# First dot products 14 tiles later, the first three column tiles multiplied pass by pass over pairs of channel tiles, and the parameters loaded behind x

## The chip, the cores and the metric

The kernel runs on one core of a Trainium2 chip. The metric is the device time of one execution in microseconds (us); the times shown are medians of several executions. The engines named below are TensorE (PE, with its weight loads as PEld), VectorE (DVE), ScalarE (ACT), GpSimd (POOL) and SyncE (SP), which issues nearly all DMA transfers.

## What is computed

One inference step of a two-layer backbone over 640 tokens (128 of a prompt, 512 of a sample), width 1024. Cut to what the change touches:

```python
def trunk_layer(x, mod_vec, rope, init, l, p):
    shift, scale, gate = split(silu(mod_vec) @ w_mod[l] + b_mod[l], 3)
    h = rms_norm(x, norm_g[l]) * (1 + scale) + shift
    proj = h @ w_in[l]              # 92 column tiles of 128, and 16 columns ca/cb
    ...                             # four mixers, each forward and backward:
    #  A retention, B RG-LRU, C gated DeltaNet (cq ck cv cz ca cb), D HGRN2 (dq df di dz)
    yb = einsum(branches, w_branch[l])
    y = sum(sigmoid(mg) * yb) @ w_out[l]
    return x + gate * y             # and the mixers' final states
```

A final RMS norm follows the second layer. The prompt and the sample have a modulation vector each (`c_ctx`, `c`), so every channel has two values of shift, scale and gate.

## The kernel before

**Tiling.** Everything is held transposed: channels on the 128 partitions, 640 tokens along the free side. `h` is eight tiles of 128 channels (KD = 8). For precision each operand of a product is split in a high part, rounded to fp32r, and a low part, the rest: `hh`, `hl` for h, `whi`, `wlo` for a weight tile. A column tile of 128 output channels is then `hi·hh + hi·hl + lo·hh`, summed over the eight channel tiles in PSUM, in two halves of 384 and 256 tokens: 48 matmuls (`product`, L363 to L391). ACT makes `whi` (L360), DVE makes `wlo` (L361); the buffers for raw weights, high and low parts are two each.

**Jobs.** `layer_jobs` yields jobs, one for a column tile: first the small one of ca and cb (16 columns, two passes only, no low part), then ck, cq, cv, dq, df, df, di and so on. `drive` takes them in, up to three ahead, and runs them. Beside them run two lanes of mixer work, whose pieces the loop places by a clock of its own; gate tiles (mg) fill in and are written out to memory where the next mixer's tiles have no buffer.

**What sets the order.** The kernel's text gives each instruction a priority, the earlier the higher. A list scheduler with a model of the times then builds each engine's queue: of those instructions whose inputs are ready in the model and whose buffer has come round (the tiles of one tag are given out in the order of the text), an engine takes the earliest in the text. So a late instruction that is ready goes ahead of an early one that is not. On the chip each engine works its queue off in that fixed order. `issue_after`, `behind` and `Ordered` (whose instructions show line L104) add edges by hand: while `ordered('V', True)` holds, the DVE instructions of the text keep their order among themselves.

**The start.** `first_h` (L663 on) makes h of layer 0, in tokens of a hand-written order: `x` loads a tile of x and adds its square, `T` and `B` make the norm's factor, `l` loads eight tiles of modulation rows, `m` multiplies them on PE, `p` transposes the result on PE and computes two tiles' worth of shift and scale, `y` normalises a tile in place, `n` makes its high part on ACT (L650), `o` its low part on DVE, `P` computes constants from the parameters (`prepare`, some 55 small DVE operations in one chain, with a few ACT operations that wait for them). The head ends with y0 and y1; the rest stands in eight steps, one for each channel tile. The first three jobs (ca/cb, ck, cq) form a group that runs with these steps: after each step, the group's matmuls of that channel tile are issued for all three jobs. In the trace their PSUM tiles have the name `wide`. ca/cb gets the 1024-column tile, ck the two banks of tag `pj`, cq those of `m1`; the fourth job, cv, needs a bank of tag `pj`.

**The dots.** The gates of both layers and the shift and scale of layer 1 don't come from PE but from DVE: `mod_dots` (L607) loads two tiles of 128x512 of `w_mod` (`wm`, three buffers) and makes four multiply-and-sum operations (`mjunk`, L613), each with an accumulator read behind it. There are 24 such steps in layer 0 and 8 in layer 1, 128 dots in all. The first step calls `cond_silu` (L595), which loads the two vectors in four pieces (`cs<-in_cvec`) and needs four tiles of the mixers' tag `pu` (11 buffers) for their tanh (`cth`, L602, on ACT; L603 on DVE). `layer_jobs` takes one step of dots with every third job:

```python
EVERY, done = 3, 0
...
                done += 1
                if done % EVERY == 0:
                    next(extra, None)
                yield j
```

Of the kernel before, what the change touches and what calls it, by code (L numbers as in the profile page):

```python
# [79 lines left out]
def hybrid_kernel(ctx: ExitStack, tc: tile.TileContext, I, O):  # L80
# [89 lines left out]
    cs0 = cp.tile([128, KD, 2], F32, name="cs0")  # L170
    nc.sync.dma_start(cs0, I['ccol'])
    par = cp.tile([128, NPAR], F32, name="par")
    nc.sync.dma_start(par, I['params'])
    ident = cp.tile([128, 128], F32, name="ident")
    con = cp.tile([128, NCON], F32, name="con")
    lvm = cp.tile([128, 5, 32], U8, name="lvm")
# [128 lines left out]
    tick = [lambda: None]  # L305
    clock = [0.0]
    held = [0]
    wide, wide_step = [], []
    zout = [0, 0]

    def free(n, z=False):
# [34 lines left out]
    def split_w(j, raw, spare=False, lo_on=None, after=[]):  # L346
        if spare:
            hi, lo = Parts(), Parts(3 - int(spare))
            for i in range(2):
                r = raw[:, 4 * i:4 * i + 4]  # L350
                A.activation(hi.tiles[i], r, AF.Copy)
                V.tensor_sub(lo.tiles[i], r, hi.tiles[i].bitcast(F32))
            return hi, lo
        if j.m < 128:
            both = w_tile(j, F32R, "hi", 1)
            A.activation(both[:, :, :16], raw, AF.Copy)
            V.tensor_sub(both[:, :, 16:], raw, both[:, :, :16].bitcast(F32))
            return both, None
        hi, lo = w_tile(j, F32R, "hi", 2), w_tile(j, F32R, "lo", 2)
        A.activation(hi, raw, AF.Copy)  # L360
        behind(lambda: (lo_on or j.lo_on or V).tensor_sub(lo, raw, hi.bitcast(F32)), after)  # L361
        return hi, lo

    def product(hi, lo, rh, rl, evac, nk=8, k0=0, halves=HALVES, tag="pj", after={}):


        m = hi.shape[-1]

        def passes(ps, k, a, b):
            ops = ((hi, rh), (hi, rl), (lo, rh))[:3 if lo else 2]  # L370
            for n, (w, r) in enumerate(ops):
                PE.matmul(ps[:m, :b - a], w[:, k0 + k], r[k][:, a:b], start=(k + n == 0), stop=(k == nk - 1 and n == len(ops) - 1))  # L372
        if wide:
            pss = [wide.pop(0) for _ in halves]
            for k in range(nk):
                for (a, b), ps in zip(halves, pss):
                    passes(ps, k, a, b)
                yield
            for (a, b), ps in zip(halves, pss):
                evac(ps[:m, :b - a], a, b)  # L380
            return
        for a, b in halves:
            ps = psp.tile([128, 512], F32, tag=tag, name="pj", bufs=2)
            for k in range(nk):
                behind(lambda: passes(ps, k, a, b), [after[k]] if k in after else [])
                clock[0] += (3 if lo else 2) * (b - a) / 2400
                tick[0]()
            evac(ps[:m, :b - a], a, b)
            yield
# [9 lines left out]
    def drive(jobs, ahead):  # L399


        q = []
        more = True

        def prepare_next(i, spare=False, lo_on=None, after=[]):
            if len(q) > i and len(q[i]) == 2 and q[i][0].deep >= i:
                j, lo = q[i]
                q[i] = j, lo, split_w(j, lo, spare, lo_on, after)
                if j.prep:
                    j.prep()  # L410

        def fill(n):
            nonlocal more
            while more and len(q) < n:
                j = next(jobs, None)
                if j is None:
                    more = False
                elif j == 'flush':
                    break
                else:  # L420
                    x = j, load_w(j)
                    if j.urgent and len(q) > 1 and len(q[-1]) == 2:
                        q.insert(-1, x)
                    else:
                        q.append(x)
                    if j.pre:
                        j.pre()
        while True:
            fill(ahead + 1)
            for i in range(3):  # L430
                prepare_next(i)
            if q:
                j, _, w = q.pop(0)
                if j.group:
                    n = j.group
                    fill(n - 1)
                    runs = [j.run(*w)]
                    for i in range(n - 1):
                        prepare_next(i, lo_on=None if n < 3 or wide_step else V, after=[edge['v0']] if n == 3 and 'v0' in edge else [])
                    for i in range(n - 1):  # L440
                        j, _, w = q.pop(0)
                        runs.append(j.run(*w))
                    if wide_step:
                        x = psp.tile([128, 1024], F32, tag="m21", name="wide", bufs=1)
                        wide.extend((x[:, :512], x[:, 512:]))
                        for tag in 'pj m1'.split():
                            wide.extend(psp.tile([128, 512], F32, tag=tag, name="wide", bufs=2) for _ in range(2))
                        f = wide_step.pop()
                        for k in range(KD):
                            behind(lambda: [next(r) for r in runs], f(k))  # L450

                        fill(1)
                        prepare_next(0, 1)
                        for r in runs[1:]:
                            next(r, None)
                    for r in runs:
                        if n == OG and n < 3 and r is runs[-1]:
                            fill(2)
                            prepare_next(0)
                            prepare_next(1, 2)  # L460
                        next(r, None)
                    fill(ahead + 1)
                    for r in runs:
                        for _ in r:
                            pass
                else:
                    for _ in j.run(*w):
                        pass
            elif not more:
                return  # L470
# [191 lines left out]

    def first_h():  # L663

        head, steps = 'x0 x1 x2 x3 x4 x5 x6 x7 l0 T m0 B p0 y0 y1'.split(), \
            [s.split() for s in 'l1 l2 l3 n0 n1 o0 m1|o1 p1 y2 y3 w1|n2 n3 o2 m2|o3 p2 y4 y5 w2|n4 n5 o4 m3|o5 p3 y6 y7 w3|n6 n7 o6|o7 P'.split('|')]
        csil = sLt[:, :256].rearrange("p (k c) -> p k c", k=KD)
        V.memset(csil, 0.0)
        th = small_tile([128, KD, 2], "cth", 1)
        A.activation(th, cs0, AF.Tanh, scale=0.5)  # L670
        V.scalar_tensor_tensor(csil[:, :, 0:2], th, 1.0, cs0, op0=OP.add, op1=OP.mult)
        nc.sync.dma_start(ident, I['ident'])
        rows, stat, xs, hh, hl = {}, {}, {}, [], []
        pm = M2(1024)
        two = up.tile([128, 2, T], F32, tag="hcb", name="two", bufs=1)
# [1 line left out]
        def load_x(k):  # L677
            if not xs:
                stat['ss'] = U(name="ss", on=1)
            xs[k] = U(name="x0", on=2)  # L680
            nc.sync.dma_start(xs[k], I['xT'][k])
            sum_sq(xs[k], stat['ss'], len(xs) == 1)

        def rms():
            stat['dg'] = stream_stat(stat['ss'], NT, two[:, 0])
# [46 lines left out]
            late.append(h_low(0, k, xs[k], 0, T, hh[k], hl[k]).ins)  # L732

        def do(tok):
            {'x': load_x, 'T': lambda n: rms(), 'B': lambda n: rms_bc(), 'l': load_rows, 'm': shift_scale, 'p': columns,
             'y': norm_x, 'o': low_h,
             'n': high_h, 'P': lambda n: behind(prepare, [late[0], *late[-2:]])}[tok[0]](int(tok[1:] or 0))

# [769 lines left out]
    def layer_jobs(f, l, extra, after_half):  # L1508
# [45 lines left out]
        jobs = [j for k, i in order for j in inp[k](i, st[k][i])]  # L1554
        gate_jobs, branch_jobs, spill = f['merge_jobs']((0, 1, 3, 2))
        AHEAD = 2
        EVERY, done = 3, 0
        jobs += gate_jobs[:AHEAD]
        gate_jobs = gate_jobs[AHEAD:]
        while jobs or any(lanes) or any(threads):  # L1560
            need = held[0] + sum((lanes[n] or threads[n]) != [] and not zout[n] for n in range(2))
            r = [t[1] for n in range(2) for t in [runnable(n)] if t]
            if extra_jobs:
                j = extra_jobs.pop(0)
            elif jobs and need + jobs[0].cost <= NPU - (RS if gate_jobs else 0):
                j = jobs.pop(0)
            elif gate_jobs and len(gate_jobs) > 8 - AHEAD and need < NPU and not (r and min(r) <= clock[0]):
                gate_jobs.pop()
                j = spill(AHEAD + len(gate_jobs))
            else:  # L1570
                j = None
            if j:
                held[0] += j.cost
                done += 1
                if done % EVERY == 0:
                    next(extra, None)
                yield j
            else:
                r = [(t[1], n, t) for n in range(2) for t in [runnable(n)] if t]
                if r:  # L1580
                    step(*min(r, key=lambda x: x[:2])[1:])
                else:
                    yield 'flush'
# [224 lines left out]
```

## Time and profile before

| | us |
|---|---|
| median of three executions | 2085.4 (2082.83 to 2087.55) |
| profiled execution, its own time | 2088.14 |
| profiled execution, span of its trace | 2086.3 |
| PE busy in the span | 2027.3 |
| DVE busy | 1401.3 |
| ACT busy | 909.3 |

The time of an execution and the span of its trace differ by 1.84 us: the span runs from the first to the last instruction. PE is busy for nearly all of it, but not in its first 120 us: the page's strip of forty slices of 52 us shows PE at 6 and 7 tenths in the first two and at 9 or more later. So the table says what the kernel is made of, and the first tenth of the span has to be read by itself, stretch by stretch.

### The profile page before, as it was taken

Reading aid. Unit: us, or ns where it says so; the run is one execution under the profiler, and the core shown is the slowest. Engines: PE = TensorE matmul, PEld = TensorE weight load, DVE = VectorE, ACT = ScalarE, POOL = GpSimd, SP = SyncE. Lnnn points to the kernel's source line nnn. Section 1 sums busy time; section 2 is a strip of 40 time slices with the busy share of each in tenths; the row PEclk is TensorE's granted clock in tenths of the full one; section 3 lists DMA queues with packets and bytes.
Section 4 is the critical chain, followed back from the end, with each engine's and each line's share of the span. In section 5 each row is a group of like instructions: output and inputs, shape, how many; then the busy total and the mean of one; then the engine's idle time right before and its main releaser. Section 6 shows DMA issues by size and latency. Waiting matters only on the chain.

```text
span 2086.3 us, 42690 instructions
## 1 busy us (share of the span) xinstructions
PE 2027.3 (97%) x17362; PEld 1983.7 (95%) x17362; DVE 1401.3 (67%) x3164; ACT 909.3 (44%) x1940; POOL 75.6 (4%) x195
## 2 busy tenths in 40 slices
PE   6799999999999999999999999999999999999997
PEld 5789999999999999999989999999999999999997
DVE  6999767866766855447567746855784686552775
ACT  4343464454445444422344435453644554362221
POOL 0000000000000000000000000000000000000000
PEclk9999999999999999999999999999999999999999
DMA  8544423323233232456322322332322233243642
GB/s 322 177 149 159 136 93 95 93 72 110 87 94 105 74 110 85 160 172 194 135 80 84 95 82 80 99 99 77 122 83 87 79 115 94 95 156 113 216 126 96
DMA packets 133305, 245.25 MB, mean 118 GB/s; under 512 B 44068, under 2 KB 59124, under 8 KB 132980
## 3 DMA queue, kind: packets, MB, share of 16 engines
q1 hardware_dynamic: 131956, 239.90, 35.6%
q8 instruction: 136, 2.23, 0.5%
q10 hardware_dynamic: 1152, 2.62, 0.3%
q14 instruction: 61, 0.50, 0.1%
HBM read 205.20 MB, written 37.27 MB: 116 GB/s over the span
## 4 chain that ended last, share of the span: by engine, by line
PE 86%; DMA 6%; DVE 4%; ACT 2%; issue 1%; SPq 1%; POOL 0%; DVEq 0%; ACTq 0%; POOLq 0%
PE pj L372 71%; PE m L298 13%; PE m L302 2%; DMA R<-gc 1%; DMA wss<-in_w_ss 1%; DVE mjunk L613 1%; DMA wm<-in_w_mod 1%; DMA sW<-l_dr 1%; DVE wlo L361 0%; DMA l_dr<-at 0%; DMA cs<-in_cvec 0%; DVE cs L835 0%; DMA tab<-in_tables 0%; DMA x<-in_xT 0%; ACT whi L360 0%
## 5 line engine op out<-in xcount | busy, mean ns | idle before, releaser
L372 PE MATMUL pj<-hh,whi 128*128 128x256 f32 (+2 forms) x2896 | 915.8, 316 | 13.0 <-ACT p_df L504 10.3
L372 PE MATMUL pj<-hl,whi 128*128 128x256 f32 (+2 forms) x2896 | 905.6, 313 | 0.0
L372 PE MATMUL pj<-hh,wlo 128*128 128x256 f32 (+1 forms) x2880 | 899.5, 312 | 0.0
L372 PEld LDWEIGHTS pj<-hh,whi 128*128 128x128 f32 (+1 forms) x2896 | 549.0, 190 | 18.0 <-ACT p_df L504 10.8
L372 PEld LDWEIGHTS pj<-hl,whi 128*128 128x128 f32 (+1 forms) x2896 | 549.2, 190 | 1.5 <-DVE hl L104 0.3
L372 PEld LDWEIGHTS pj<-hh,wlo 128*128 128x128 f32 x2880 | 546.8, 190 | 1.4
L361 DVE TENSOR_TENSOR wlo<-wraw,whi 128x1024 fp32r<-128x1024 f32 x228 | 278.7, 1222 | 162.1 <-ACT whi L360 158.8
L360 ACT ACTIVATE whi<-wraw 128x1024 fp32r<-128x1024 f32 x230 | 243.4, 1058 | 325.9 <-PE pj L372 291.2
L372 PE MATMUL pj<-bl,whi 128*128 128x384 f32 (+1 forms) x512 | 158.3, 309 | 0.0
L372 PE MATMUL pj<-bh,whi 128*128 128x384 f32 (+1 forms) x512 | 158.0, 309 | 0.0
L372 PE MATMUL pj<-bh,wlo 128*128 128x384 f32 (+1 forms) x512 | 157.8, 309 | 0.0
L372 PEld LDWEIGHTS pj<-bh,whi 128*128 128x128 f32 x512 | 96.4, 188 | 0.0
L372 PEld LDWEIGHTS pj<-bh,wlo 128*128 128x128 f32 x512 | 96.3, 188 | 0.0
L372 PEld LDWEIGHTS pj<-bl,whi 128*128 128x128 f32 x512 | 96.2, 188 | 0.0
L504 ACT ACTIVATE mg<-pj 128x384 f32<-128x384 f32 (+1 forms) x128 | 54.9, 429 | 87.0 <-PE pj L372 83.2
L613 DVE SCALAR_TENSOR_TENSOR mjunk<-wm,cs 128x512 bf16<-128x512 f32 x128 | 87.6, 684 | 2.6 <-DMA wm<-in_w_mod 2.2
L372 PE MATMUL pj<-yl,whi 128*128 128x256 f32 (+1 forms) x256 | 78.9, 309 | 0.0
L372 PE MATMUL pj<-yh,whi 128*128 128x384 f32 (+1 forms) x256 | 78.7, 310 | 0.0
L372 PE MATMUL pj<-yh,wlo 128*128 128x256 f32 (+1 forms) x256 | 78.0, 309 | 0.0
L526 ACT ACTIVATE junk<-m 128x128 bf16<-128x128 f32 x160 | 44.3, 277 | 73.7 <-PE m L298 62.9
L947 DVE TENSOR_TENSOR sW<-sW,sLt 128x126 f32<-128x126 f32 (+22 forms) x248 | 62.7, 253 | 12.1 <-ACT hkst L1161 3.9
L949 DVE TENSOR_TENSOR sW<-sW 128x126 f32<-128x126 f32 (+22 forms) x248 | 62.6, 252 | 4.6
(394 smaller groups left out, 2916.9 us busy)
## 6 DMA issues: line engine op xcount, KB each, us to landing
wraw<-in_w_in SPq DMA_DIRECT2D x184, 512.0 KB
mg<-mg SPq DMA_DIRECT2D x96, 320.0 KB
wm<-in_w_mod SPq DMA_DIRECT2D x64, 256.0 KB
wraw<-in_w_branch SPq DMA_DIRECT2D x32, 512.0 KB
R<-gc SPq DMA_DIRECT2D x32, 320.0 KB
braw<-br SPq DMA_DIRECT2D x32, 320.0 KB
wss<-in_w_ss SPq DMA_DIRECT2D x32, 256.0 KB
wraw<-in_w_out SPq DMA_DIRECT2D x16, 512.0 KB
```

The source lines that it names most:

```text
L298: return PE.matmul(out, lhsT, rhs, **k)
L302: return PE.transpose(out, in_, idn)
L360: A.activation(hi, raw, AF.Copy)
L361: behind(lambda: (lo_on or j.lo_on or V).tensor_sub(lo, raw, hi.bitcast(F32)), after)
L372: PE.matmul(ps[:m, :b - a], w[:, k0 + k], r[k][:, a:b], start=(k + n == 0), stop=(k == nk - 1 and n == len(ops) - 1))
L504: A.activation(dst[:, a:b], ps, AF.Tanh, scale=0.5)
L526: A.activation(junk, src3[:, t, :], AF.Square, accum_out=ss[:, t:t + 1])
L613: V.scalar_tensor_tensor(junk, w, 1.0, cs[2 * g + a], op0=OP.mult, op1=OP.mult, accum_out=macc[l][:, c, 2 * g + a:2 * g + a + 1])
L947: V.tensor_tensor(tv, X3[:, :m, i:i + 1].to_broadcast([128, m, n]), L3[:, i:i + 1, i + 1:].to_broadcast([128, m, n]), op=OP.mult)
L949: V.tensor_tensor(X3[:, :m, i + 1:], X3[:, :m, i + 1:], tv, op=OP.subtract)
```

## The change

1. `done` starts at -14 in layer 0 (0 in layer 1), and no step of dots is taken while it is negative: the first is taken with the fourteenth job instead of the third, and `cond_silu` with it.
2. In the group of three, the steps are taken in pairs of channel tiles. After the first step of a pair the pass hi·hh is issued for both tiles and all three jobs, then the pass hi·hl; after the second step, behind the PE transpose that it names, the pass lo·hh. The jobs are started in the order ck, cq, ca/cb, so that ck gets the 1024-column tile, cq the `pj` banks and ca/cb the `m1` banks.
3. The low parts of ck's and cq's weights (`wlo`) are not made before the group begins but after the first pair's first two passes in the text, so behind h's low parts o0 and o1, and ahead of p1, y2, y3 in DVE's order by hand. The tokens are rearranged: both low parts of a pair in one step, and `m` at the beginning of the next.
4. The parameters (170 KB) and the identity (64 KB) are loaded by a new token `i` behind x7 and ahead of l0; they were ahead of x.

```diff
-    nc.sync.dma_start(par, I['params'])
...
-    wide, wide_step = [], []
+    wide, wide_step, lows = [], [], []
...
-        behind(lambda: (lo_on or j.lo_on or V).tensor_sub(lo, raw, hi.bitcast(F32)), after)
+        def low():
+            behind(lambda: (lo_on or j.lo_on or V).tensor_sub(lo, raw, hi.bitcast(F32)), after)
+        if wide_step:
+            lows.append(low)
+        else:
+            low()
...
         if wide:
             pss = [wide.pop(0) for _ in halves]
-            for k in range(nk):
-                for (a, b), ps in zip(halves, pss):
-                    passes(ps, k, a, b)
-                yield
+            ops = ((hi, rh), (hi, rl), (lo, rh))
+            for p in range(0, nk, 2):
+                for n, (w, r) in enumerate(ops):
+                    for k in (p, p + 1) if w else ():
+                        for (a, b), ps in zip(halves, pss):
+                            PE.matmul(ps[:m, :b - a], w[:, k], r[k][:, a:b], start=(k + n == 0),
+                                      stop=(k == nk - 1 and n == (2 if lo else 1)))
+                    yield
...
-                        for k in range(KD):
-                            behind(lambda: [next(r) for r in runs], f(k))
+                        for p in range(KD // 2):
+                            f(2 * p)
+                            for n in range(2):
+                                for r in runs[1:] + runs[:1]:
+                                    next(r)
+                            if p == 0:
+                                for x in lows:
+                                    x()
+                                lows.clear()
+                            edges = f(2 * p + 1)
+                            behind(lambda: [next(r) for r in runs], edges)
...
-        head, steps = 'x0 x1 x2 x3 x4 x5 x6 x7 l0 T m0 B p0 y0 y1'.split(), \
-            [s.split() for s in 'l1 l2 l3 n0 n1 o0 m1|o1 p1 y2 y3 w1|n2 n3 o2 m2|o3 p2 y4 y5 w2|n4 n5 o4 m3|o5 p3 y6 y7 w3|n6 n7 o6|o7 P'.split('|')]
+        head, steps = 'x0 x1 x2 x3 x4 x5 x6 x7 i l0 T m0 B p0 y0 y1'.split(), \
+            [s.split() for s in 'l1 l2 l3 n0 n1 o0 o1|m1 p1 y2 y3 w1|n2 n3 o2 o3|m2 p2 y4 y5 w2|n4 n5 o4 o5|m3 p3 y6 y7 w3|n6 n7 o6 o7|P'.split('|')]
...
-        nc.sync.dma_start(ident, I['ident'])
...
+        def load_params():
+            nc.sync.dma_start(par, I['params'])
+            nc.sync.dma_start(ident, I['ident'])
...
-        EVERY, done = 3, 0
+        EVERY, done = 3, 0 if l else -14
...
-                if done % EVERY == 0:
+                if done >= 0 and done % EVERY == 0:
```

## Rows read from the trace of the kernel before

**Rows 1.** The page, busy time, share of the span and instructions of each engine.

```profile
PE 2027.3 (97%) x17362; PEld 1983.7 (95%) x17362; DVE 1401.3 (67%) x3164; ACT 909.3 (44%) x1940; POOL 75.6 (4%) x195
```

**Rows 2.** Busy time by stretch: start and end, length, each engine, granted clock, DMA.

```profile
24.44:53.85 29.41, 24.98 (x287) 21.91 (x283) 24.86 (x63) 11.77 (x23) 1.87 (x11) 1.00 0.85 314
...
86.66:96.72 10.06, 0.00 (x2) 0.00 (x1) 9.50 (x42) 1.86 (x5) 0.00 (x0) 0.74 0.56 181
96.72:101.50 4.78, 4.78 (x15) 4.78 (x16) 4.78 (x29) 0.22 (x1) 0.00 (x0) 0.50 0.54 164
...
112.43:114.92 2.49, 0.00 (x0) 0.00 (x1) 2.49 (x8) 0.24 (x1) 0.00 (x0) 1.00 0.32 105
114.92:118.60 3.68, 3.68 (x39) 3.46 (x43) 3.58 (x12) 0.47 (x2) 0.00 (x0) 0.56 0.89 275
...
131.00:150.00 19.00, 17.04 (x186) 16.33 (x186) 18.30 (x49) 8.99 (x22) 1.01 (x5) 1.00 0.47 151
```

**Rows 3.** The waits of PE, first 60 us (total, times, longest).

```profile
PE wide L372 <- DVE hl L104: 2.4, 2, 1.3
PE wide L372 <- ACT hh L650: 1.9, 1, 1.9
PE pj L372 <- ACT p_ck L491: 1.4, 1, 1.4
```

**Rows 4.** The waits of all engines, 86 to 97 us.

```profile
PE pj L372 <- ACT p_df L504: 10.1, 1, 10.1
ACT scr L219 <- DVE scr L218: 6.0, 1, 6.0
```

**Rows 5.** The timeline of DVE: start, duration, line, operation, tiles.

```profile
51.89 0.91 DVE L104 MEMSET sLt<- 128x1024 f32 x1 [0.16 <-issue]
...
83.25 0.69 DVE L613 SCALAR_TENSOR_TENSOR mjunk<-wm,cs 128x512 bf16<-128x512 f32 x1
...
83.87 0.17 DVE L104 SCALAR_TENSOR_TENSOR scr<-scr,scr 128x16 f32<-128x16 f32 x1
...
102.05 0.16 DVE L104 TENSOR_SCALAR ghh<-par 128x2 f32<-128x2 f32 x1
```

**Rows 6.** The dots, 44 to 131 us: durations least/median/most, first, last.

```profile
L613 DVE SCALAR_TENSOR_TENSOR mjunk<-wm,cs x68: 627/685/694, 44.9 to 127.8; 128x512 bf16<-128x512 f32 x68
```

**Rows 7.** The loads of xn, tokens of x for the output tiles.

```profile
L1469 SPq DMA_DIRECT2D xn<-in_xT x8: 333/386/1745, 954.7 to 1035.6; - x8
```

**Rows 8.** The timeline of ACT: where the eleventh job is evacuated.

```profile
142.88 0.26 ACT L490 ACTIVATE p_cv<-pj 128x128 f32<-128x128 f32 x1
```

**Rows 9.** The timeline of DVE: low weight parts, first dot.

```profile
24.46 2.35 DVE L104 TENSOR_TENSOR wlo<-wraw,whi 128x1024 fp32r<-128x1024 f32 x2
...
44.90 0.68 DVE L613 SCALAR_TENSOR_TENSOR mjunk<-wm,cs 128x512 bf16<-128x512 f32 x1
```

**Rows 10.** The timeline of SP, and the chain that ended last.

```profile
1.20 0.42 SPq L173 DMA_DIRECT2D par<-in_params  x1
...
2.13 4.29 SPq L681 DMA_DIRECT2D x<-in_xT  x8
...
5.25 6.41 DMA x<-in_xT
...
29.31 5.34 DMA wss<-in_w_ss
```

**Rows 11.** The timeline of PE at full clock, two matmuls on.

```profile
80.00 0.33 PE L372 MATMUL pj<-hh,whi 128*128 128x384 f32 x1
80.17 0.33 PE L372 MATMUL pj<-hl,whi 128*128 128x384 f32 x1
```

**Rows 12.** Busy time by stretch, as in rows 2, while dots still run.

```profile
150.00:240.00 90.00, 90.00 (x728) 89.31 (x727) 87.69 (x248) 32.25 (x70) 1.72 (x4) 1.00 0.49 154
```

**Rows 13.** The timeline of DVE: two steps of the first triangular solve.

```profile
149.82 0.18 DVE L947 TENSOR_TENSOR sW<-sW,sLt 128x31 f32<-128x31 f32 x1
...
189.81 0.27 DVE L947 TENSOR_TENSOR sW<-sW,sLt 128x110 f32<-128x110 f32 x1
```

More of the change, by code (lines that the diff above doesn't have):

```diff
@@ L734, in do @@
         def do(tok):
-            {'x': load_x, 'T': lambda n: rms(), 'B': lambda n: rms_bc(), 'l': load_rows, 'm': shift_scale, 'p': columns,
+            {'x': load_x, 'i': lambda n: load_params(), 'T': lambda n: rms(), 'B': lambda n: rms_bc(), 'l': load_rows, 'm': shift_scale, 'p': columns,
              'y': norm_x, 'o': low_h,
```

## Prediction

> **What bounds the kernel now.** I read the page first: PE is busy for 97% of the span [rows 1], so apart from waits the kernel takes as long as its matmuls, and the change takes none away. What it can win is idle time of PE and time at the lower clock. Next I cut the first 160 us into stretches by busy time and granted clock [rows 2], then asked in each which wait ended last [rows 3, 4], and last read what VectorE (DVE) and ScalarE (ACT) did there [rows 5]. Four places matter.
>
> The products with h run from 24.44 to 53.85 us. Of these 29.41 us PE is busy for 24.98, so 4.43 us are idle [rows 2]: two waits for low parts of h, 2.4 us, and one for a high part, 1.9 us [rows 3]. Behind the group cv waits another 1.4 us for ck's evacuation to free a `pj` bank [rows 3].
>
> From 86.66 to 96.72 PE stands still for 10.06 us and comes back at a granted clock of 0.50, the lower of the two levels (1.2 of 2.4 GHz), for 4.78 us [rows 2]. The wait is for the evacuation of a df tile, which ACT could have done; but ACT, working its queue in order, stood 6.0 us at an exponential that waits for DVE, and then at another [rows 4]. The operand is the end of a chain of small DVE operations of 0.17 us. That chain is `prepare` and then the softplus of the gates, and it needs from 51.89 to 102.05 us [rows 5], because its next operation is never ready when the last one ends: DVE slips a dot of 0.69 us in between each time [rows 5]. By 131 us 68 of the 128 dots have run [rows 6], although the text gives most of them a place far later.
>
> From 112.43 to 114.92 PE waits 2.49 us more, for `g`, at the end of the same softplus chain, and again runs slowly afterwards, at a mean clock of 0.56 for 3.68 us [rows 2]. From 131 to 150 it idles for 19.00 - 17.04 = 1.96 us.
>
> **Dots later.** Priority alone moves nothing, since the scheduler takes whatever is ready. What holds the dots back is a buffer: `cond_silu` needs four tiles of tag `pu`, and a tag's tiles are given out in the order of the text. The trace bears that out: the loads of xn need only a buffer and are not issued before 954.7 us [rows 7]. With the fourteenth job three ahead, the four tiles come behind those of the eleventh job, cv of the second head, evacuated at 142.88 us now [rows 8], some 20 us earlier once the stalls below are gone. So dots begin near 120 us in place of 44.90 [rows 9].
>
> First stall: chain and softplus have no dots between them. Some 55 operations of 0.17 to 0.25 us and the lane's own work end by about 70 us, ahead of ACT's need. 10.06 us go, and the slow stretch: 15 matmuls in 4.78 us are 0.319 each, 0.17 at full clock [rows 2, 11], so 2.2 to 2.4 us; I take 4.78 x (1 - 0.50) = 2.4. Sum -12.5. If the model's queue puts those exponentials ahead of an evacuation again, some of it stays: bound -6.
>
> Second stall: -2.49 and 3.68 x (1 - 0.56) = 1.6, so -4.1; bound 0, if `g` is still late.
>
> The dots' new place: the 60 dots after 131 us stand beside 1.96 us of idle PE from 131 to 150 [rows 2] and none from 150 to 240, with DVE nearly full [rows 12]: 0.033 us each at most. At that rate 128 cost 4.2, so +2.2 net of the 1.96 already paid. Lower bound: +0 - 2.0 (they cost nothing). Upper: the 68 early dots stood beside 12.5 + 4.1 = 16.6 us, 0.24 each; 128 x 0.24 = 31, +29 net. I take the lower rate, because the later dots are those that ran beside the same mixers. Their 64 loads of `wm` and four of the vectors stay on SP's queue, and weight loads queue behind them there as they do now; that is in the rate. The four `cth` tiles take turns in a tag of 11 whose next tiles (ak, aq) wait behind them: each needs a tanh and a multiplication of dot size, so four times about 1.4 us, an estimate from the dot's 0.69 [rows 5]. Two PSUM banks of the running products hide it; uncovered it would be 5 to 6.
>
> **The group of three.** The 4.43 us of idle time have three causes. First PE waits about 1.3 us for hl [rows 3], which stands on DVE behind two wlo of together 2.35 us [rows 9]; the new order puts o0 and o1 first, and the two passes hi·hh and hi·hl need no wlo. The two later waits (1.9, and 2.4 - 1.3 = 1.1) come from the four vector operations of `cond_silu` and the first dots, which start at 44.90 [rows 9] in the midst of y6 and y7; they leave with the dots. So up to -4.43.
>
> The x transfers: par and the identity are two issues, 2.13 - 1.20 = 0.93 us [rows 10]; x's eight tiles, 2.62 MB, take 6.41 us, 409 GB/s [rows 10], so 234 KB are 0.6 us. I take -0.6 (0 to -0.93): the chain x, squares, norm, y, n begins that much earlier. The parameters are needed only after m0, so their later landing is hidden by l0's 2.1 MB; uncovered it would cost the same 0.6.
>
> A new wait: on DVE p1, y2, y3 now stand behind both wlo (2.35 us), and the pass lo·hh waits on PE for p1's transpose. PE has there the two passes, 24 matmuls or about 3.4 us, the rest of m1 and what of m2 has landed, against about 2 us for o0 and o1 and 2.35 for the wlo: +0.6 (0 to 2). Later pairs have 2.9 us of products and 2 us of m to cover 4 us of y, n, o, and I see no wait. Sum of the group: -4.4 (0 to -6).
>
> cv's first wait: cq, not ck, now holds the `pj` banks, and its evacuation stands behind ck's on ACT, 0.4 us later; but ca/cb, with no third pass, and ck are finished before the group ends, so their evacuations are over sooner. I take 0.9 us of wait instead of 1.4, -0.5 (+0.7 to -1.3).
>
> Where TensorE runs first after long idling, the clock matters. The stretch from 24.44 is at 1.00 throughout [rows 2], though PE waited at the start. The Trainium skill, "TensorE: Matmul & The Clock Gate", section "What's actually happening", says that the throttled clock is the default and that activity releases it. By that rule the first products, which now come earlier, would run at 1.2 GHz for a while. Priced as the stretch after the second stall, 1.6 us, the rule would make the sum -17.7; the row, 1.00, doesn't bear it out, and the sum goes without it.
>
> **The sum.** -12.5 - 4.1 + 2.2 - 4.4 - 0.5 = -19.3 us. The profiled execution took 2088.1 us (span 2086.3 and 1.8 around it): 2068.8. The median is 2.7 below that execution: 2085.4 - 19.3 = 2066.
>
> **Rivals.** All on the median.
> - *The dots don't move.* If the tag's tiles went to whoever is ready, `cond_silu` would run where it runs now and the chain would stay broken up. Only group, cv and x remain, -4.9, perhaps less: 2080. Against it: rows 7. 0.08.
> - *The start wins nothing.* Modulation rows land until 29.31 + 5.34 = 34.65 us [rows 10] whatever the order, and strict order on DVE could make new gaps. Without the 4.4: 2070.5. Against it: after 30 us PE, not the transfers, sets the pace. 0.12.
> - *Half of the first stall stays*, because an exponential of the chain still stands ahead of an evacuation in ACT's queue: +6, 2072. 0.09.
> - *Slower: the dots break another chain.* The second head's triangular solve is 62 dependent DVE operations of some 0.25 us. In the first solve eighteen of them took from 149.82 to 189.81 us beside dots [rows 13], 2.2 us each. If dots begin at 120 and still run at the next solve, or meet the first one's inverse, whose results PE needs, 128 dots at 0.24 cost 31: 2085.4 - 21.5 + 29 = 2093. It decides above (21.5 + 2.0) / 128 = 0.18 us a dot. Against it: 0.033 in the stretch after 131. 0.08.
> - *First products at the lower clock*, by the mechanism of the second stall's aftermath: +1.6, 2068. It is what the skill's rule above would give. 0.03.
>
> **Chances and range.** The forecast has 0.60: its terms' favourable bounds (-6, -1.3, -2.0 for the dots) reach 2059, its unfavourable ones with part of a stall about 2074. The range reaches on to the rivals with 2070 to 2080: 2057 to 2080 leaves out the slower case and a few hundredths on each side, under 0.2. A measurement of this kernel tells 0.2%, 4.2 us, from no change. Faster: forecast, start, half stall, clock, and half of the unmoved dots at 2080, 0.88; same: the other half, 0.04; slower 0.08.
>
> **What would show it.** Right: the first `mjunk` after 110 us; the chain that ends in `ghh` over by 75; no wait of PE above 2 us from 50 to 110 and granted clock 1.00 there; `wide` ending near 49.5; x's first tile 0.6 earlier; the last dot between 280 and 350 us with PE full. Wrong: dots at 45 us, a long wait of PE behind ACT or for `fo`, `at` or `g`, gaps in `wide` at the transposes, or more idle time of PE from 120 to 350 than 4 us.

## The result, and the profile after

| us | before | after |
|---|---|---|
| median of four executions | 2086.35 (2082.83 to 2087.55) | 2064.07 (2062.44 to 2065.67) |
| profiled execution, span | 2086.3 | 2060.7 |
| PE busy in the span | 2027.3 | 2021.5 |
| PE idle in the span | 59.0 | 39.2 |

The changed kernel takes 0.9896 of the time before, with a 95% interval from 0.9879 to 0.9913: 22.3 us less between the medians, where 19.3 less were forecast. (The kernel before has one execution more here than in the table ahead of the prediction.) Between the two profiled executions the span is 25.6 us shorter: 19.8 of it are idle time of PE and 5.8 are busy time, which shrinks because stretches at the lower clock are gone: the two of [rows 2], worth 4.0 by the prediction's reckoning, and later ones (the kernel before reads 0.98 from 700 to 800, 1000 to 1100 and 1300 to 1400 us, the changed one 0.97 from 1200 to 1300 us and 1.00 in the other hundreds between 400 and 2000).

The page of the changed kernel, engines' busy time, answers to [rows 1]; the number of matmuls is the same:

```profile
PE 2021.5 (98%) x17362; PEld 1979.1 (96%) x17362; DVE 1403.5 (68%) x3164; ACT 907.9 (44%) x1940; POOL 75.7 (4%) x195
```

Where the idle time went is seen by stretch. Idle PE before and after: from 0 to 55 us 20.2 and 17.0; from 55 to 160 us 14.7 and 0.7; from 160 to 400 us 3.3 and 2.3; behind that 20.8 and 19.3. So 14.0 of the 19.8 us lie where the two stalls were. The windows of the changed kernel, with the columns of [rows 2]; the first is that of the products with `wide`:

```profile
24.04:50.67 26.63, 25.47 (x288) 21.77 (x284) 20.33 (x53) 9.31 (x20) 2.13 (x11) 1.00 0.86 318
60.00:80.00 20.00, 19.90 (x142) 19.70 (x140) 14.44 (x79) 9.25 (x33) 1.42 (x7) 1.00 0.12 43
80.00:100.00 20.00, 19.92 (x141) 19.68 (x141) 15.22 (x38) 9.26 (x24) 0.17 (x3) 1.00 0.32 98
100.00:120.00 20.00, 19.49 (x279) 18.33 (x278) 19.84 (x46) 11.09 (x24) 1.40 (x8) 1.00 0.40 127
131.00:150.00 19.00, 19.00 (x216) 18.10 (x215) 18.80 (x58) 8.99 (x20) 0.00 (x0) 1.00 0.49 146
160.00:400.00 240.00, 237.70 (x2166) 230.92 (x2165) 215.27 (x569) 112.48 (x261) 10.44 (x24) 1.00 0.48 148
```

The granted clock (the column before the last two) reads 1.00 in each, and from 60 to 100 us DVE is no longer full. The waits of PE in the first 160 us (total, times, longest) hold all that is left of [rows 3, 4]:

```profile
PE m L297 <- DMA wss<-in_w_ss: 13.4, 3, 12.9
PE pj L376 <- ACT p_cq L508: 2.1, 1, 2.1
PE wide L384 <- ACT hh L667: 1.2, 1, 1.2
PE m L297 <- ACT sq L922: 0.5, 1, 0.5
PE m L297 <- DVE mod L104: 0.3, 1, 0.3
```

Read against [rows 3]: both waits for `hl`, 2.4 us together, are gone; the wait for `hh` went from 1.9 to 1.2; cv's wait for a free bank went from 1.4 to 2.1 and now names cq. The 10.1 us behind `p_df` of [rows 4] and the 2.49 us for `g` have no successor. The first row's 12.9 us is the start of the kernel, before any modulation row has landed.

The timeline of DVE shows the chain of [rows 5] from its memset to `ghh`, and behind it the end of the softplus, `g`:

```profile
47.77 0.91 DVE L104 MEMSET sLt<- 128x1024 f32 x1 [0.16 <-issue]
...
73.73 0.16 DVE L104 TENSOR_SCALAR ghh<-par 128x2 f32<-128x2 f32 x1
...
75.66 0.20 DVE L817 TENSOR_TENSOR g<-sp,ea 128x40 f32<-128x40 f32 x1
```

It takes 26 us where it took 50. The dots, with the columns of [rows 6] (durations, first and last start), stand behind it:

```profile
L630 DVE SCALAR_TENSOR_TENSOR mjunk<-wm,cs x128: 649/685/694, 105.1 to 304.8; 128x512 bf16<-128x512 f32 x128
```

### The profile page after: what moved, and what is told of

Its sections match the earlier page's. It is cut to its first block, busy times and chain, and to the rows that moved or that the text cites. A ratio compares the mean times of both kernels' runs of the same rounds, so it can differ in the third digit from the quotient of the medians.

```text
span 2060.7 us, 42665 instructions
## 1 busy us (share of the span) xinstructions
PE 2021.5 (98%) x17362; PEld 1979.1 (96%) x17362; DVE 1403.5 (68%) x3164; ACT 907.9 (44%) x1940; POOL 75.7 (4%) x195
## 4 chain that ended last, share of the span: by engine, by line
PE 89%; DVE 5%; DMA 3%; ACT 2%; issue 1%; SPq 1%; POOL 0%; DVEq 0%; ACTq 0%
PE pj L376 73%; PE m L297 13%; PE m L301 2%; DVE mjunk L630 1%; PE wide L384 1%; DMA wss<-in_w_ss 1%; DMA R<-gc 1%; DVE wlo L361 1%; DMA dct<-d_dr 0%; DMA sW<-l_dr 0%; DMA par<-in_params 0%; DVE cs L855 0%; ACT dfull L1002 0%; ACT whi L359 0%; DMA wm<-in_w_mod 0%
```

## Experiments

The theory at the start: the time comes from the dots leaving the two chains, their new place costs little, and the group's edit gives a few us on top. Its rival: the group's edit and the order of the loads bring a good part of it. Later a third theory was needed, on the order of the queues.

**1. Dots alone.** The kernel before with the dots' edit and nothing else:

```diff
-        EVERY, done = 3, 0
+        EVERY, done = 3, 0 if l else -14
...
-                if done % EVERY == 0:
+                if done >= 0 and done % EVERY == 0:
```

> The kernel before with one edit alone: the dots begin with the fourteenth job. If the gain is the dots' (theory), the two stalls between 86 and 119 us go with their slow stretches, 14 to 18 us of the 22; the start keeps its waits for hl, and the waits behind y6 and y7 shrink because the four vector operations and first dots have left: 2066 to 2072. Rival, that the group's order is needed for it (a wait of PE stays between 50 and 110 us): above 2076.

Measured: 2073.24, ratio 0.9948 (0.9930 to 0.9966), 12.9 us faster than before and a little above what was expected (its seven executions run from 2071.95 to 2079.77). The dots start at 105.6 us and both stalls are gone, so the mechanism holds. But it is 9 us slower than the whole change, more than the group was priced at. The windows of this kernel from 200 to 280 us, and PE's waits from 200 to 290, show idle time and a lower clock:

```profile
200.00:240.00 40.00, 37.28 (x369) 35.80 (x368) 35.69 (x95) 16.12 (x36) 0.00 (x0) 0.96 0.57 175
240.00:280.00 40.00, 35.83 (x239) 34.91 (x238) 37.21 (x100) 14.68 (x35) 1.56 (x1) 0.91 0.55 180
```

```profile
PE m L298 <- DVE gS L1075: 2.3, 1, 2.3
PE m L298 <- DVE r L1048: 1.8, 1, 1.8
PE m L298 <- ACT um L994: 1.6, 1, 1.6
PE pj L372 <- DVE p_bz L499: 1.1, 1, 1.1
```

The first three are results that the first head's inverse and state hand from DVE and ACT to PE. The whole change has them in the same 80 us with 1.5 us of idle time and a clock of 1.00. Why, was not clear here.

**2. All but the dots.** The whole change with `done` at 0 and its test as before.

> The changed kernel with the dots back at every third job from the beginning. Theory: only the group's gain remains, 3 us at most, and the chain of small operations is broken up by dots again, with a wait of PE near 10 us behind ACT: 2080 to 2086. Rival, that the new order of the start also frees the chain: below 2074.

Measured: 2084.12, ratio 0.9992 (0.9980 to 1.0004). Waits of PE from 60 to 130 us, and the row of the dots:

```profile
PE pj L376 <- ACT p_df L521: 12.3, 1, 12.3
PE m L297 <- DVE g L817: 2.8, 1, 2.8
```

```profile
L630 DVE SCALAR_TENSOR_TENSOR mjunk<-wm,cs x128: 625/684/711, 47.3 to 239.1; 128x512 bf16<-128x512 f32 x128
```

Both stalls are back, and with the dots early the rest of the change cannot be told from nothing. The rival falls. PE does come to the first stall sooner (the job behind cv starts at 61.64 us, in the kernel before at 63.72), but then waits 2.2 us longer for `p_df`.

**3. A buffer of its own for the gates' `cth`.** The whole change, but the four tiles come out of the weights' tag `wm` instead of the mixers' `pu`:

```diff
-UP([128, 512], name="cth")
+up.tile([128, 512], F32, tag="wm", name="cth", bufs=3)
```

> The changed kernel, dots still at the fourteenth job in the text, but the four tanh tiles of the dots' vectors take buffers of the dots' own tag (wm) in place of the mixers' tag pu. Theory, that the queue of buffers of pu holds the dots back and not their place in the text: the first dot runs between 40 and 60 us again, the wait of PE behind ACT returns, 2078 to 2088. Rival, that the place in the text does it: first dot near 105 us and 2062 to 2066.

Measured: 2090.88, ratio 1.0031 (1.0020 to 1.0042). The text is that of the whole change, yet the dots start at 50.3 us, PE waits 8.2 us behind `p_df` and 2.6 for `g`, and the gain is gone. So the place in the text does not hold the dots back; the queue of `pu` buffers does, as the prediction had it. It comes out 0.3% above the kernel before, a little more than expected. Part of that stands at the start: cv begins at 58.09 us and the job behind it at 66.78, 3.1 us later than in the kernel before.

**4. ck's banks first.** In the changed kernel cq's evacuation frees cv's bank. Here the jobs start in the old order, so that ck has the `pj` banks again:

```diff
-                                for r in runs[1:] + runs[:1]:
+                                for r in runs:
```

> The changed kernel with the jobs of the group started in the order ca/cb, ck, cq as before, so that ck and not cq holds the two pj banks that cv waits for. In the changed kernel cv waits 2.1 us for cq's evacuation, which stands on ACT behind ck's and a table load. Theory, that the banks cause that wait: it shrinks to about 0.5 us and the kernel gains 1 to 2 us. Rival, that the waiting only moves (ACT or the split of cv's weights is late anyway): within 0.5 us of the changed kernel.

Measured: 2071.37, ratio 0.9926 (0.9909 to 0.9944). cv's longest wait shrank from 2.1 to 0.7 us and its first matmul stands at 51.13 instead of 54.00 us, as wanted; but the kernel is 7 us slower than the changed one. The loss is from 200 to 280 us, with the waits of experiment 1 (`r` 2.2, `gS` 2.1, `um` 1.8 us), and 3.15 us are idle from 320 to 360. The expectation missed: what was won at the start was worth nothing at the end. It was also less than the 2.9 us by which cv starts earlier, because ten small matmuls of another tile, 1.28 us in all, now stand behind cv's beginning instead of ahead of cv; the job behind cv starts 1.8 us earlier, at 59.72 instead of 61.51.

**5 to 7. No dots at all.** Three kernels from which the dots are taken out: the changed kernel, that of experiment 4, and the kernel before.

```diff
+    for l in range(DEPTH):
+        G.memset(macc[l], 0.0)
...
-            w = up.tile([128, 512], F32, tag="wm", name="wm", bufs=3)
-            nc.sync.dma_start(w, I['w_mod'][l, c, :, 512 * a:512 * a + 512])
...
-                V.scalar_tensor_tensor(junk, w, 1.0, cs[2 * g + a], op0=OP.mult, op1=OP.mult,
...
-        cs = cond_silu()
+        cs = None
```

> The changed kernel with the 128 dots, their loads and the four tanh pieces left out (the gates of both layers and layer 1's shift and scale then come from the bias alone). What the dots still cost in their new place is the changed kernel less this. Theory, a few hundredths of a us each as in the trace of before after 131 us: 2059 to 2063. Rival, that they still slow the mixers' chains as early ones did (0.24 us each, 31 in all): below 2040.

> The variant with ck in the pj banks, also without dots. It was 7 us slower than the changed kernel, with PE waiting 200 to 280 us for the first head's inverse and state chain, where dots run. Theory, that the dots beside that chain are its loss: without them it equals the changed kernel without dots or is 1 to 2 us faster, as cv starts sooner: 2057 to 2062. Rival, that another order of the queues after the bank swap costs the 7 us by itself: 5 us or more slower than the changed kernel without dots.

> The kernel before without dots, loads and tanh pieces (gates and layer 1's shift and scale from the bias alone). What the dots cost where they stood is the kernel before less this. Theory, the two stalls with their slow stretches and the waits of y6 and y7, 17 to 21 us: 2065 to 2069. Rival, that something else breaks the chain of small operations up as well: above 2073.

Measured: 2058.72, ratio 0.9867 (0.9852 to 0.9881); 2066.86, ratio 0.9908 (0.9894 to 0.9921); 2065.37, ratio 0.9903 (0.9888 to 0.9918). Number 5 is 0.3 us below its range, number 7 within its own, and number 6 came out as its rival had it. Between the medians the dots cost 2064.07 - 2058.72 = 5.3 us in their new place, 0.042 each (6.0 by the ratios, whose intervals leave some 3 us either way). In the old place, with the kernel before at 2086.78 in the same series, they cost 21.4, 0.167 each. That agrees with the first theory's mechanism. But each of these subtractions also compares two orders of the queues, and that weighs as much as the small number: by the ratios, the late dots cost 3.8 us in experiment 4 (less number 6), and in the kernels of experiments 1 and 9 to 12 below, less number 5 or 7, anything from 0.8 to 20.4. All of it lies below the rival's 31; how much of it is the dots and how much the order isn't shown.

The three kernels among themselves have no dots, and differ all the same: the rest of the change gains 6.7 us without dots (number 7 less number 5), and with the jobs in the old order (number 6) it gains nothing. Number 6 is 8 us slower than number 5, as experiment 4 is 7 us slower than the changed kernel, but not in the same place. PE has no idle time from 200 to 280 us in either, and the waits for `r`, `gS` and `um` don't occur; from 55 to 400 us it idles for 11.1 us in experiment 4 and 3.7 in number 6. So those waits of experiment 4 come only where dots run beside that chain, as the theory of number 6 said, and a loss of like size arises elsewhere by the order alone: against number 5, number 6 has 1.5 us more idle time up to 55 us, 1.8 from 55 to 160, 2.1 from 400 to 600 and 1.9 behind. Its longest wait of PE between 20 and 60 us is for ck's evacuation:

```profile
PE pj L376 <- ACT p_ck L508: 3.1, 1, 3.1
```

ACT's timeline shows what stands in the way: a load of the activation table for the logarithm of `lg`, between two parts of ck's evacuation. Load and logarithm take 1.4 of the 3.1 us. Yet the job behind cv starts at 62.54 us, in number 5 at 63.10, so this wait doesn't explain the 8 us.

```profile
51.88 0.25 ACT L507 ACTIVATE p_ck<-wide 128x128 f32<-128x128 f32 x1
52.15 1.28 ACT L245 ACT_TABLE_LOAD   x1
53.45 0.21 ACT L245 ACTIVATE lg<-rz 128x16 f32<-128x16 f32 x1
53.57 0.37 ACT L508 ACTIVATE p_ck<-wide 128x256 f32<-128x256 f32 x1
```

**8. Dots still later.** The changed kernel with -30 in place of -14.

> The changed kernel with the first dots at the thirtieth job instead of the fourteenth. Theory, that the dots cost what the chain costs that they stand beside: they begin near 200 us, beside the first head's inverse and state chain, and PE waits for it: 3 to 10 us slower than the changed kernel. Rival, that anywhere behind the start is as good: within 2 us of it.

Measured: 2068.05, ratio 0.9914 (0.9900 to 0.9927). The dots run from 285.3 to 485.7, later than expected, and 4.2 us of PE are idle from 400 to 600 where the changed kernel has none; 1.7 are idle from 100 to 120 (0.5 in the changed kernel), where no dot runs. It is 4.0 us slower, as the theory said, but not beside the chain that the theory named. Later is not simply better.

**9 to 12. Neighbours.** If the 9 us between experiment 1 and the whole change are the group's, they must show wherever the dots begin. So the dots' start was set to -11 and -17, without and with the rest of the change.

> The kernel before with the dots alone moved, to the eleventh job. The changed kernel is 9 us faster than the one with the dots alone moved to the fourteenth, although cv starts 1.1 us earlier there. Theory, that these 9 us are the luck of the queues' order around the first head's inverse and state chain (200 to 290 us) and not the group's edit: the four neighbours (with and without the group's edit, eleventh and seventeenth job) scatter by 5 us or more and some without the edit come below 2068. Rival, that the group's edit is worth 9 us: the two without it stay near 2073, the two with it near 2064.

> The kernel before with the dots alone moved, to the seventeenth job. Theory, luck of the order: anywhere from 2062 to 2076, with the difference from its neighbour in idle time of PE between 200 and 400 us. Rival, the group's edit is worth 9 us: 2071 to 2075.

> The changed kernel with the dots at the eleventh job. Theory, luck of the order: anywhere from 2060 to 2074. Rival, the group's edit is worth 9 us wherever dots begin: 2062 to 2066.

> The changed kernel with the dots at the seventeenth job. Theory, luck of the order: anywhere from 2060 to 2074. Rival, the group's edit is worth 9 us wherever dots begin: 2062 to 2066.

| dots' start | dots alone | with the rest of the change |
|---|---|---|
| -11 | 2069.50, 0.9929 (0.9917 to 0.9941) | 2075.92, 0.9965 (0.9952 to 0.9978) |
| -14 | 2073.24, 0.9948 (0.9930 to 0.9966) | 2064.07, 0.9896 (0.9879 to 0.9913) |
| -17 | 2063.06, 0.9907 (0.9893 to 0.9921) | 2069.51, 0.9930 (0.9916 to 0.9943) |

The rest of the change gains 9 us at -14 and loses 6 at each neighbour (at -17 the two intervals just overlap); the mean of the three is 2068.6 without it and 2069.8 with it. So a fixed gain of 9 us falls, and any fixed gain of more than a few us with it. The theory held, except that -11 with the rest came out 2 us above its range. The windows from 240 to 280 us say where much of the difference arises; first dots alone at -17, then the whole change at -11, with its waits of PE from 200 to 290 us:

```profile
240.00:280.00 40.00, 40.00 (x288) 39.97 (x287) 38.48 (x84) 23.78 (x44) 2.27 (x2) 1.00 0.55 182
```

```profile
240.00:280.00 40.00, 34.21 (x220) 32.80 (x219) 39.13 (x104) 14.41 (x33) 1.17 (x1) 0.87 0.55 170
```

```profile
PE m L297 <- DVE r L1068: 2.7, 2, 1.6
PE m L297 <- DVE vk L1079: 2.1, 1, 2.1
PE m L297 <- ACT um L1014: 1.1, 1, 1.1
```

PE has no idle time there in one order, and 5.8 us with a clock of 0.87 in the other; from 55 to 400 us, which takes in most of what the orders move about, it idles for 3.4 and 8.4. What in the list scheduler makes a given text fall one way or the other was not settled. The order of loads and the later `wlo` were not tried alone.

## Why the prediction was right, and where it was not

**The dots move: right.** They start at 105.1 where 120 was estimated. The evacuation from which the estimate was made starts at 125.52 us instead of 142.88 [rows 8], some 17 us earlier where 20 were said; but DVE used the first `cth` at 103.81, so the buffers had come round before that evacuation, not behind it. That the tag holds them back is shown by experiment 3. Of the signs that were to show the forecast right, three missed by little: the first `mjunk` came before 110 us, one wait of PE above 2 us stands at 54.00, and `wide` ended at 50.67 and not near 49.5.

**Two stalls, -16.6: right.** Idle PE from 55 to 160 fell by 14.0; the prediction's idle terms there are 10.06, 2.49 and 1.96, together 14.5. Its clock terms are 2.4 and 1.6, and from 60 to 150 us the clock reads 1.00 in every window shown; busy time fell by 5.8 over the whole span. The chain was to be over by 75 us and ended at 73.73, the softplus at 75.66. The rival in which half of the first stall stays did not occur.

**The dots' new place, +4.2 gross: not contradicted, but not measured so finely.** The subtraction gives 5.3 to 6.0 for this kernel, and from 0.8 to 20.4 for others with late dots. So the rival's 31 us fall, and the rate of 0.033 us a dot is one that an order can reach, not a price that holds. Dots alone at -11, -14 and -17 gain 14.0, 12.9 and 20.4 us, where the prediction's terms for the dots alone, -16.6 + 2.2, make 14.4.

**The group and cv, -4.4 - 0.5: wrong.** This is the step that failed: "Sum of the group: -4.4", and with it "0.9 us of wait instead of 1.4". Idle time inside the products fell from 4.43 to 26.63 - 25.47 = 1.16 us, and they ended at 50.67 instead of 53.78. So 3.1 us were won there, of 4.4. But cv started at 54.00 instead of 55.15, 1.15 us earlier, and PE waits 2.1 us there where 0.9 were expected. The job behind cv starts at 61.51 instead of 63.72: 2.2 us reached it, of the 4.9 that the two terms make. The difference between 1.15 and 2.2 is for the most part ten small matmuls, `m<-sel,cab`, which run in the midst of cv in the kernel before (first two rows) and ahead of cv in the changed one (last two):

```profile
60.03 1.28 PE L298 MATMUL m<-sel,cab 32*128 32x16 f32 x10
63.72 0.34 PE L372 MATMUL pj<-hh,whi 128*128 128x384 f32 x1
```

```profile
50.60 1.28 PE L297 MATMUL m<-sel,cab 32*128 32x16 f32 x10
61.51 0.41 PE L376 MATMUL pj<-hh,whi 128*128 128x384 f32 x1
```

The timeline of ACT shows who took the rest, and that of PE its effect:

```profile
51.36 0.36 ACT L508 ACTIVATE p_ck<-wide 128x256 f32<-128x256 f32 x1
51.62 0.36 ACT L510 ACTIVATE p_ck<-wide 128x256 f32<-128x256 f32 x1
52.00 1.28 ACT L245 ACT_TABLE_LOAD   x1
53.29 0.21 ACT L245 ACTIVATE lg<-rz 128x16 f32<-128x16 f32 x1
53.41 0.26 ACT L507 ACTIVATE p_cq<-wide 128x128 f32<-128x128 f32 x1
53.57 0.38 ACT L508 ACTIVATE p_cq<-wide 128x256 f32<-128x256 f32 x1
```

```profile
54.00 0.44 PE L376 MATMUL pj<-hh,wpart 128*128 128x384 f32 x1 [2.12 <-ACT p_cq L508]
```

`prepare` now runs its logarithm just as the evacuations are due, and its table load stands between ck's and cq's; load and logarithm move cq's evacuation from 52.0 to 53.41 us, 1.4 of the 2.1 us of wait. In the kernel before, that load began at 48.93 us and ACT was idle for 3.41 us behind it, so it cost nothing. So the step left out was in cv's wait: the prediction counted the evacuations on ACT and not what `prepare` puts between them. The Trainium skill, "ScalarE: Activation LUTs", section "What ACT_TABLE_LOAD costs", gives 1283 ns for the load and another 1380 ns for a drain. The row has 1.28 us, as the page says; the drain isn't seen, since the operation before ended at 51.98 and `lg` began at 53.29.

Moreover most of the group's gain was the dots'. With the dots alone moved, the products with `wide` end at 51.05 us (-14), 51.77 (-11) and 51.45 (-17); with the rest of the change at 50.67, 50.92 and 50.68. So the rest wins 0.4 to 0.9 us in the group, and the dots' move alone 2.0 to 2.7. Behind cv the two are mixed: the next job starts at 62.96, 62.13 and 61.81 us without the rest, at 61.51, 62.96 and 62.74 with it (the clock over cv read 0.83, 1.00, 1.00 and 1.00, 0.80, 0.80). The prediction had said that two of the three causes leave with the dots, but entered them under the group; only the 1.3 us for `hl` were the group's own, and they did go: 1.3 us is still the longest wait for `hl` in experiment 1. In its place stands a wait of 1.2 us for `hh`, which is 0.2 us with the dots alone moved.

**The loads, -0.6.** ACT's first square of x starts at 4.31 us instead of 6.47, so 2.2 us earlier, but the first product at 24.04 instead of 24.44. Not even these 0.4 are shown to be the loads': experiment 1 has the old order of loads and its first product at 24.05, and the kernels with the new order run from 23.40 (experiment 8) to 24.70 (experiment 3).

**Low clock at the first products: did not occur, but for another reason.** From 24.04 to 50.67 the granted clock is 1.00, though PE waited 12.9 us at the start. The prediction took these products for PE's first work and held the row against the rule of the Trainium skill, "TensorE: Matmul & The Clock Gate", section "What's actually happening". They aren't: PE runs small matmuls from 12.93 us on. The trace's record of the clock begins at 21.61 us, with the full clock, in the kernel before at 19.76; a window ahead of that prints 1.00 because it has no record. The durations there show the lower level. First the changed kernel, then the kernel before:

```profile
15.74 3.21 PE L297 MATMUL m<-wss,sLt 128*32 128x128 f32 x56
18.89 2.50 PE L297 MATMUL rps<-two,ones 128*128 128x128 f32 x10
21.92 0.88 PE L297 MATMUL m<-wss,sLt 128*32 128x128 f32 x24 [0.32 <-DVE mod L104]
```

```profile
19.58 1.45 PE L298 MATMUL rps<-two,ones 128*128 128x128 f32 x10
```

The same matmul of `wss` takes 0.057 us each before the record begins and 0.037 after, and the ten of `rps` take 2.50 us ahead of the rise and 1.45 where the rise comes at their beginning. So this case agrees with the rule: the work behind the long wait ran slowly, only it was this small work, and the clock had risen before the first product. The rival's price of 1.6 us for the products rightly stayed out of the sum, and the reason that the prediction gave for it was wrong.

**What the prediction did not have.** Orders that do the same work differ by up to 13 us (2063.06 to 2075.92 in the table), and experiments 5 and 6 by 8 without any dots. Its slower rival, dots that break another chain, was priced at 31 us; where those chains did wait, as in experiments 1, 4 and 11, PE idled for 6.9 to 7.5 us from 200 to 280 us, against 1.5 in the changed kernel. So the total of 2066 has the right size because its large terms, the two stalls, are right. That it came within 3 us is in good part luck: the same terms would give nearly the same time for -11 and -17, where the whole change gains 7.6 and 14.0 us, and the 2.7 us that the group and cv fell short are covered by the fall of this one order, which is no term of the sum.

## What to carry to other kernels

Work that may run late, and is always ready, slips into every gap of a chain of short dependent operations; hold it back by something that the scheduler must obey, here a buffer that comes round late, and price it by its rate beside the engine that sets the end, not by its own duration; here that rate came out anywhere from 0.006 to 0.16 us a dot, with the order. When a job starts earlier, see what was moved behind it before calling that a gain. When a stage ends earlier, look at what else becomes ready at that moment on the engine that must clear its results, table loads too. Where a list scheduler builds the queues, try neighbours of the chosen number before a few us are put down to an edit: here the same edit gained 9 and lost 6.

## What the runs showed of the hardware that was not expected

A table load of 1.28 us on ACT between two evacuations took, with the logarithm behind it, 1.4 us of a wait of PE: of 2.1 us in the changed kernel and of 3.1 in experiment 6. And waits of only 1 to 3 us each stood beside a mean granted clock of 0.91 (experiment 1) and 0.87 (experiment 11) from 240 to 280 us, where the two orders with little or no waiting, the changed kernel and dots alone at -17, read 1.00. Such a mean is a stretch at the lower level: in experiment 11 the clock reads 0.50 from 255.94 to 266.18 us, which begins within the second of two waits for `r`, of 1.1 and 1.6 us. But the fall doesn't always come. Behind the same wait of 2.1 us for cq's evacuation, cv and the few matmuls up to the next job read 1.00 in the changed kernel and 0.80 in experiment 11, and took 1.2 us longer:

```profile
54.00:61.51 7.51, 7.41 (x50) 7.21 (x50) 5.50 (x14) 4.01 (x8) 0.00 (x0) 1.00 0.39 133
54.24:62.96 8.72, 8.72 (x49) 8.72 (x50) 6.52 (x19) 3.84 (x7) 0.00 (x0) 0.80 0.34 112
```

Experiments 8 and 12 read 0.80 there too. What decides it isn't shown.
